# Sixty-four column products of a conditioning matrix shared out over three engines, in the filter stage of a gMLP/Hyena block

## The chip, the cores and the metric

One core of a Trainium2 chip. The metric is the device time in microseconds (us) of one execution; the runs before the change have a median of 2732.48 us (three runs, 2732.22 to 2733.73).

## The reference, cut to what matters

The block computes, for 512 tokens of width 2048 in float32:

```python
mod = silu(c) @ w_ada + b_ada                    # 6 vectors of 2048: sh1, sc1, g1, sh2, sc2, g2
h   = x * (1 + sc1) + sh1
z   = h @ w_in + b_in                            # 2048 -> 9216, then split
# Hyena branch: filters of length 512, made from positions alone
f   = sin(fr * (feats @ w1 + b1)); f = sin(fr * (f @ w2 + b2)); f = f @ w3
filt = f.reshape(L, 2, 2, 1024) * window         # direction, order, channel
y = x2 * conv(x1 * conv(v, filt0) + skip0, filt1) + skip1     # by a transform of length 1024
# then the gating branch, w_o, LayerNorm, a 2048 -> 8192 -> 2048 MLP, LayerNorm
```

All that the change touches lies before the first product with `w_in`: the vectors sh1 and sc1, the filters, and h.

## The kernel before, in words

**Number format.** A float32 product is made of float32r parts: a value is split into a high part (a cast on ScalarE, ACT) and a low part (value minus high, on VectorE, DVE), and three matmuls of high and low parts are added up. A block of weights (128x1024) so costs a cast (`whi`, L164) and a subtraction (`wlo`, L169), and the matmuls that take its low part wait for the subtraction.

**The modulation.** sh1 and sc1 aren't made on TensorE (PE). Each chunk of 128 columns, in two halves, is a tile `araw` of 128x1024; `Modulation.step` multiplies it with the broadcast silu(c) (`cond`) and adds up along the row, in one DVE instruction (L289, "a step" below). There are 64 steps for sh1 and sc1: 2 vectors, 16 chunks, 2 halves. After each fourth step one chunk of h can be made by `first_input`: two small POOL additions (`mod`, L295 and L296), two ACT instructions (the high part `act`, L476, and the full value in place in `xT`, L477), and one POOL subtraction (the low part, L478). So sixteen such chunks, kc 0 to 15.

**The filters.** Two sines (`Sine`: a matmul, an ACT scaling, `reduce` with six DVE instructions, an ACT Sin) give `a2`. Then eight parts, n = 0 to 7, each with three stages: `taps(n)` on PE (12 matmuls, and in even parts one more, L437, that adds the skip weight to the first tap), `windowed(n)` on DVE (four products of a PSUM bank with the window, L445), and `transform(n)` on PE (6 float32 matmuls, in the profile 12 rows: f_ee, f_eo, and two f_o of two matmuls each). The sums of part n (six DVE instructions, L376, L354 or L356, L380) read the transform's banks. PSUM has eight banks, used in turn: `taps` and `transform` have four each, so `transform(n)` overwrites what sums(n-1) read, and `taps(n+1)` what `windowed(n-1)` read. The loop over n issues taps(n+1), transform(n), two steps, windowed(n+1), the stores of the part before, the split of the next filter weights (`w3h`, `w3l`, each second part), sums(n).

**The first product.** Then two column groups of `w_in` are computed together, in sixteen blocks b0 to b15 of 24 matmuls; block b(2k) and b(2k+1) use the chunks kc 2k and 2k+1 of h. The loop over u = 0 to 15 issues on DVE: some of the remaining steps, all done by u = 12, then the `wlo` of block u+1; on PE: block u. In-order queues set all of this: every engine runs its instructions in the written order, and a waiting instruction holds up what stands behind it.

`busy(n)` issues n transposes of an identity whose result nobody reads. After u = 15 the program goes on with short convolutions, the other column groups and all the rest, which the change leaves as it is.

Of the kernel before, what the change touches and what calls it, by code (L numbers as in the profile page):

```python
# [11 lines left out]
F32 = mybir.dt.float32  # L12
F32R = mybir.dt.float32r
AF = mybir.ActivationFunctionType
OP = mybir.AluOpType
# [3 lines left out]
P = 128  # L19
# [21 lines left out]
def block_kernel(ctx: ExitStack, tc: tile.TileContext, t):  # L41
    nc = tc.nc
    const = ctx.enter_context(tc.tile_pool(name="const", bufs=1))
# [3 lines left out]
    small = ctx.enter_context(tc.tile_pool(name="small", bufs=2))  # L47
# [18 lines left out]

    def f32(ap):
        return ap.bitcast(F32)

    def load(dst, src, queue=nc.sync):  # L70
        queue.dma_start(dst, src)
        return dst

    def split(src, hi, lo):

        nc.scalar.copy(hi, src)
        nc.vector.tensor_tensor(lo, src, f32(hi), op=OP.subtract)
# [165 lines left out]
    cond = const.tile([P, D], F32, name="cond")  # L243
# [7 lines left out]
    sign = const.tile([P, 1], F32, name="sign")  # L251
    nc.gpsimd.memset(sign[:HID], 1.0)
    nc.gpsimd.memset(sign[HID:], -1.0)
    first_tap = const.tile([1, P], F32, name="first_tap")
    nc.gpsimd.memset(first_tap, 0.0)
    nc.gpsimd.memset(first_tap[:, 0:1], 1.0)
    ident = const.tile([P, P], F32, name="ident")
    make_identity(nc, ident)

    def busy(n):  # L260

        ps = bank("busy")
        for _ in range(n):
            nc.tensor.transpose(ps[:, :P], ident, ident)


    dots = const.tile([P, 6, KC, 2], F32, name="dots")
    mod = const.tile([P, 6, KC], F32, name="mod")

    class Modulation:  # L270
        def __init__(self, order, room=lambda: 0):

            self.order, self.raw, self.room = [(m, kc, h) for m, kc in order for h in range(2)], [], room

        def load(self):
            early = sum(r[0] for r in self.raw)
            more = early < min(self.room(), 8)
            if self.order and (more or len(self.raw) - early < 3):
                m, kc, h = self.order.pop(0)
                if more:  # L280
                    raw = actp.tile([P, 1024], F32, name="araw", tag="act")
                else:
                    raw = wts.tile([P, 1024], F32, name="araw", tag="araw")
                load(raw, t["ada"][m, kc, h])
                self.raw.append((more, raw, m, kc, h))

        def step(self):
            _, raw, m, kc, h = self.raw.pop(0)
            nc.vector.scalar_tensor_tensor(raw, raw, 1.0, cond[:, 1024 * h:1024 * (h + 1)], op0=OP.mult,  # L289
                                           op1=OP.mult, accum_out=dots[:, m, kc, h:h + 1])  # L290
            if len(self.raw) < 11:
                self.load()

    def mod_sum(m, kc, eng=nc.vector):
        eng.tensor_tensor(mod[:, m, kc], dots[:, m, kc, 0], dots[:, m, kc, 1], op=OP.add)  # L295
        eng.tensor_tensor(mod[:, m, kc], mod[:, m, kc], bada[:, m, kc], op=OP.add)  # L296
# [87 lines left out]
    PARTS = [(o, hf, cs) for o, hf in ((1, 1), (1, 0), (0, 0), (0, 1)) for cs in range(2)]  # L384

    class Filters:
# [6 lines left out]
        def middle(self):  # L393
            x = self.one.reduce()
            nc.scalar.activation(x, x, AF.Sin)
            self.two = Sine(hw2, x, 1, P)

        def ready(self):

            x = self.two.reduce()  # L400
            nc.scalar.activation(x, x, AF.Sin)
            even, odd = slot_pair("a2e"), slot_pair("a2o")
            split(x, *even)
            for a, b in zip(even, odd):
                nc.scalar.activation(b, f32(a), AF.Identity, scale=sign)
            self.a2 = [[a.rearrange("h (p k) -> h k p", k=4) for a in pair] for pair in (even, odd)]

        def fetch(self, n):

            o, hf, cs = PARTS[n]  # L410
            if cs == 0:
                w = load(slot("w3"), t["w3"][o, hf].rearrange("d h c -> (d h) c"))
                skip = load(slot("skip")[:1], t["skip"][o, hf:hf + 1])
                self.raw.append((w, skip))
            if n in (0, 2):
                for i in (2, 3) if hf else (0, 1):
                    self.win.append(load(actp.tile([P, 1024], F32, name="win", tag="act"), t["win"][i]))

        def parts(self, n):
            if PARTS[n][2] == 0:  # L420
                w, skip = self.raw.pop(0)
                both = slot_pair("w3")
                split(w, *both)
                self.w.append((*both, skip))

        def taps(self, n):

            cs = PARTS[n][2]
            wh, wl, skip = self.w[0] if cs == 0 else self.w.pop(0)
            ah, al = self.a2[cs]  # L430
            for cl in range(4):
                ps = bank("flt")
                extra = cs == 0 and cl == 0
                for m, (a, w) in enumerate(((ah, wh), (ah, wl), (al, wh))):
                    nc.tensor.matmul(ps, a[:, cl, :], w, start=m == 0, stop=m == 2 and not extra)  # L435
                if extra:
                    nc.tensor.matmul(ps, first_tap, skip, start=False, stop=True)  # L437
                self.ps.append(ps)

        def windowed(self, n):  # L440
# [27 lines left out]

    h1 = []

    def first_input(kc, xt):

        mod_sum(slice(0, 2), kc, nc.gpsimd)
        hi, lo = act_pair(kc)
        sc, sh = mod[:, 1, kc:kc + 1], mod[:, 0, kc:kc + 1]
        nc.scalar.activation(hi, xt, AF.Identity, bias=sh, scale=sc)  # L476
        nc.scalar.activation(xt, xt, AF.Identity, bias=sh, scale=sc)  # L477
        nc.gpsimd.tensor_tensor(lo, xt, f32(hi), op=OP.subtract)  # L478
        h1.append((hi, lo))

    def short_conv(ps, which, hf):
# [16 lines left out]
    ada = Modulation(((m, kc) for kc in range(KC) for m in range(2)), lambda: KC - 2 - len(h1) - 4 * bool(windows))  # L498
# [2 lines left out]
    bada = cload("bada", (P, 6, KC))  # L501
    flt = Filters()
    flt.fetch(0)
    silu = [slot("silu") for _ in range(4)]
    quarters = [cond[:, 512 * h:512 * (h + 1)] for h in range(4)]
    for s_, c_ in zip(silu, quarters):
# [6 lines left out]
    xt = []  # L513

    def x_load():
        if len(xt) < KC:
            xt.append(load(slot("xT"), t["xT"][len(xt)]))

    done = []

    def ada_steps(n):

        for _ in range(n):
            ada.step()
            done.append(None)
            if len(done) % 4 == 0:
                first_input(len(h1), xt[len(h1)])
                x_load()

    x_load()  # L530
    ada.load()
# [1 line left out]
    for m in (1, 4):  # L533
        nc.vector.tensor_scalar(bada[:, m], bada[:, m], 1.0, None, op0=OP.add)
    busy(14)
    ada_steps(2)
    flt.parts(0)
    flt.ready()
    busy(14)
    x_load()  # L540
    for _ in range(5):
        ada.load()
    flt.taps(0)
    ada_steps(2)
    flt.windowed(0)
    weights.later, weights.queue = [], nc.scalar
    for n in range(8):
        if n < 6 and n % 2 == 0:
            flt.fetch(n + 2)
        if n < 7:  # L550
            flt.taps(n + 1)
        sums = flt.transform(n)
        ada_steps(2)
        if n < 7:
            flt.windowed(n + 1)
        flt.store()
        if n < 6:
            flt.parts(n + 2)
        sums()
        if 2 <= n < 5:  # L560
            weights.load()
        if n == 5:
            weights.cast()
        if n == 6:
            weights.finish()
            weights.cast()
# [31 lines left out]
    for x in fc.tiles:  # L598
        both = slot_pair("fc")
# [111 lines left out]
    def do(f, *args):  # L711
        return lambda: f(*args)
# [52 lines left out]
    ada = Modulation((m, kc) for m in (2, 4, 3, 5) for kc in range(KC))  # L765
# [16 lines left out]
    for cg in range(4):  # L782
# [3 lines left out]
        ps = dense(t["w_b"], cg, 4, Bp)  # L786
# [56 lines left out]
    for hf in range(2):  # L843
# [77 lines left out]
    r = [[None] * 4 for _ in TILES]  # L921
# [100 lines left out]
    skips = []  # L1022

    w_o = t["w_o"]
    early, late = (0, 1), (2, 3)
# [213 lines left out]
```

## Time and profile before

| what | us |
|---|---|
| median of three runs | 2732.48 |
| the profiled execution | 2733.2 |
| its span, first to last instruction | 2731.4 |
| PE busy | 2688.6 (98%) |
| DVE busy | 1539.5 (56%) |
| ACT busy | 777.8 (28%) |
| POOL busy | 118.8 (4%) |
| mean granted TensorE clock | 0.996 |

The profiled execution lies 0.7 us above the median, and its span leaves 1.8 us around it. Rows of the timeline give the start of an instruction, its duration, engine, line, operation, output and inputs, how many follow each other, and in brackets how long the engine was idle before it and what ended that. Durations overlap a little at their ends (a step lasts 1.22 us and the next starts 1.15 us after it). PE rows with a wait on the memory of operands are modelled, so their starts are read, not their ends. All rows are the profile's, with the line numbers of the kernel before.

### The profile page before, as it was taken

The numbers are of one execution on the slowest core, as the hardware profiler recorded it, in microseconds if no ns is written. First come the engines' busy times: TensorE is split into PE (matmuls) and PEld (weight loads), VectorE is DVE, ScalarE is ACT, GpSimd is POOL, SyncE is SP. The second block draws the span as 40 slices with busy tenths as digits, with TensorE's granted clock in tenths as the row PEclk, the third lists the DMA queues.
The fourth block names the chain that finished last, engine by engine and source line by source line (L and its number), as shares of the span: only waits on it lengthen the run. The fifth ranks groups of instructions, "written<-read, shape, count | busy, mean of one in ns | idle before, by whom it ended". The sixth has DMA issues, their size and how long they took to land.

```text
span 2731.4 us, 30019 instructions
## 1 busy us (share of the span) xinstructions
PE 2688.6 (98%) x12019; PEld 2210.1 (81%) x12019; DVE 1539.5 (56%) x2052; ACT 777.8 (28%) x949; POOL 118.8 (4%) x102
## 2 busy tenths in 40 slices
PE   8999999999999999999999999999999999999996
PEld 5678778888888888878988888888888888888885
DVE  8987989544575566456774343443433434334348
ACT  2343332222232222324621222312223222131232
POOL 0330000000000000140010000000000000000001
PEclk9999999999999999999999999999999999999998
DMA  9762333555665567445543222322223222223342
GB/s 346 300 242 84 118 113 135 196 190 196 200 209 186 198 220 258 156 152 177 183 134 100 94 100 93 101 93 100 94 99 97 96 100 93 101 92 101 95 140 82
DMA packets 120189, 400.49 MB, mean 147 GB/s; under 512 B 14187, under 2 KB 14283, under 8 KB 119920
## 3 DMA queue, kind: packets, MB, share of 16 engines
q1 hardware_dynamic: 116656, 387.26, 41.9%
q10 hardware_dynamic: 3392, 11.31, 1.1%
q8 instruction: 94, 1.54, 0.2%
q14 instruction: 47, 0.39, 0.0%
HBM read 388.01 MB, written 10.50 MB: 146 GB/s over the span
## 4 chain that ended last, share of the span: by engine, by line
PE 91%; DVE 5%; DMA 3%; issue 1%; ACT 1%; SPq 0%; DVEq 0%; ACTq 0%
PE d L207 57%; PE t L952 29%; DMA araw<-in_ada 2%; PE flt L435 1%; PE f_o L338 1%; DVE wlo L169 1%; DMA spec<-spec 1%; PE inv L703 1%; PE inv L690 1%; DMA wraw<-in_w_m 0%; PE f L342 0%; DVE araw L289 0%; DVE r L1104 0%; DVE r L968 0%; PE tr L609 0%
## 5 line engine op out<-in xcount | busy, mean ns | idle before, releaser
L207 PE MATMUL d<-act,whi 128*128 128x512 f32 (+1 forms) x4224 | 1273.1, 384 | 0.0
L169 DVE TENSOR_TENSOR wlo<-wraw,whi 128x1024 fp32r<-128x1024 f32 x480 | 589.0, 1229 | 993.2 <-ACT whi L164 989.9
L164 ACT CAST whi<-wraw 128x1024 fp32r<-128x1024 f32 x480 | 504.9, 1053 | 1488.2 <-PE d L207 873.2
L207 PEld LDWEIGHTS d<-act,whi 128*128 128x128 f32 x4224 | 783.1, 188 | 155.6 <-issue 2.4
L207 PE MATMUL d<-act,wlo 128*128 128x512 f32 (+1 forms) x2112 | 810.2, 384 | 10.2 <-DVE wlo L169 10.2
L207 PEld LDWEIGHTS d<-act,wlo 128*128 128x128 f32 x2112 | 396.7, 188 | 93.3 <-DVE wlo L169 15.9
L952 PE MATMUL t<-whi,fh 128*128 128x512 f32 x960 | 373.5, 389 | 0.0
L952 PE MATMUL t<-wlo,fh 128*128 128x512 f32 x960 | 373.5, 389 | 0.0
L952 PE MATMUL t<-whi,fl 128*128 128x512 f32 x960 | 373.5, 389 | 0.0
L289 DVE SCALAR_TENSOR_TENSOR araw<-araw,cond 128x1024 f32<-128x1024 f32 x192 | 238.6, 1259 | 7.8 <-DMA araw<-in_ada 7.6
L952 PEld LDWEIGHTS t<-whi,fl 128*128 128x128 f32 x960 | 180.2, 188 | 37.4
L952 PEld LDWEIGHTS t<-whi,fh 128*128 128x128 f32 x960 | 180.2, 188 | 37.4
L952 PEld LDWEIGHTS t<-wlo,fh 128*128 128x128 f32 x960 | 180.2, 188 | 37.4
L952 PE MATMUL t<-whi,act 128*128 128x512 f32 x512 | 159.7, 391 | 0.0
L952 PEld LDWEIGHTS t<-whi,act 128*128 128x128 f32 x512 | 96.1, 188 | 19.9
L967 DVE TENSOR_TENSOR gated<-t,cond 128x512 f32<-128x512 f32 x126 | 86.2, 684 | 31.6 <-PE t L952 31.6
L952 PE MATMUL t<-wlo,act 128*128 128x512 f32 x256 | 99.8, 390 | 2.1 <-DVE wlo L169 2.1
L968 DVE TENSOR_TENSOR r<-r,gated 128x512 f32<-128x512 f32 x126 | 87.2, 692 | 4.3
L207 PE MATMUL d<-whi,act 128*128 128x512 f32 x256 | 79.0, 389 | 0.0
L1062 DVE TENSOR_TENSOR relu<-relu 128x512 f32<-128x512 f32 (+1 forms) x68 | 45.6, 671 | 38.2 <-ACT fh L1061 38.2
L1106 POOL TENSOR_TENSOR r<-r,ln2b 128x512 f32<-128x512 f32 x6 | 10.0, 1665 | 1305.1 <-DVE r L1104 1303.8
L952 PEld LDWEIGHTS t<-wlo,act 128*128 128x128 f32 x256 | 48.1, 188 | 12.3 <-DVE wlo L169 2.5
(253 smaller groups left out, 1966.9 us busy)
## 6 DMA issues: line engine op xcount, KB each, us to landing
wraw<-in_w_m SPq DMA_DIRECT2D x264, 512.0 KB, 3.5
araw<-in_ada SPq DMA_DIRECT2D x192, 512.0 KB, 5.7
wraw<-in_w_in SPq DMA_DIRECT2D x123, 512.0 KB, 3.6
wraw<-in_w_o SPq DMA_DIRECT2D x48, 512.0 KB, 3.4
spec<-spec SPq DMA_DIRECT2D x48, 256.0 KB, 4.0
wraw<-in_w_in ACTq DMA_DIRECT2D x21, 512.0 KB, 6.7
wraw<-in_w_b SPq DMA_DIRECT2D x16, 512.0 KB, 3.6
wraw<-in_w_a SPq DMA_DIRECT2D x16, 512.0 KB, 3.4
```

Of the source, the lines that this page charges most:

```text
L164: nc.scalar.copy(hi, raw)
L169: nc.vector.tensor_tensor(lo, raw, f32(hi), op=OP.subtract)
L207: nc.tensor.matmul(out[i], a, b, start=first and m == 0, stop=last and m == 2)
L289: nc.vector.scalar_tensor_tensor(raw, raw, 1.0, cond[:, 1024 * h:1024 * (h + 1)], op0=OP.mult, op1=OP.mult, accum_out=dots[:, m, kc, h:h + 1])
L338: nc.tensor.matmul(ps, fc(k), x, start=first, stop=last)
L435: nc.tensor.matmul(ps, a[:, cl, :], w, start=m == 0, stop=m == 2 and not extra)
L690: nc.tensor.matmul(ps, ic(4 * cs + COLUMN[cl]), y[cl][cs], start=(cs == 0), stop=(cs == 1))
L703: nc.tensor.matmul(ps[:, cl * P:(cl + 1) * P], conv.y[cl][cs][:, s], ic(4 * cs + COLUMN[cl]), start=(cs == 0), stop=(cs == 1))
L952: nc.tensor.matmul(out[i], a, b, start=kc == 0 and m == 0, stop=kc == 2 * pairs - 1 and m == 2)
L967: nc.vector.tensor_tensor(x, ps[i], g2_row[c], op=OP.mult)
L968: nc.vector.tensor_tensor(r[i][c], r[i][c], x, op=OP.add)
L1062: nc.vector.tensor_tensor(x, x, x, op=OP.mult)
```

## The change

1. Of the 64 steps, 19 become two instructions: `products` multiplies on POOL (L302 of the new kernel), `add_up` copies the product in place on ACT and adds up along the row (L309). Two products are issued before the loop, then two or three in each part up to n = 6; the sums on ACT stand at the head of the next part. Six more stay DVE steps before the loop, none inside it. When the loop ends 25 steps are done (before: 20), and 39 remain for the first product (before: 44): three per u instead of three or four.
2. The small additions of `first_input` run on DVE where `add_up` triggers them, on POOL otherwise; the low part of h moves from POOL to DVE (L510). It is put in a list (`lows`) and issued by `low()`: after the next step, in the filter loop behind `windowed`.
3. The second sine's `reduce` is issued before the split of the filter weights and after one step, not after two; its Sin is computed twice on ACT, once straight into the high part.
4. `busy(14)` before the first taps becomes `busy(36)`.
5. The four skip rows are loaded once, into partitions 0, 32, 64 and 96 of one tile, split once on ACT and DVE, and added by two float32r matmuls in place of one float32 matmul.

The DVE queue around the first taps and windows, before. Names: `araw` a step, `w3l` the low part of filter weights, `a2el` that of the sines, `flt` the windowed taps:

```order
L289 SCALAR_TENSOR_TENSOR araw,dots<-araw,cond 128x1024 x2
L77 TENSOR_TENSOR w3l<-w_122,w3h 128x512
L316 TENSOR_SCALAR sine_k<-sine 128x512
L317 TENSOR_SCALAR sine_k<-sine_k 128x512
L319 SCALAR_TENSOR_TENSOR sine<-sine_k,sine 128x512 x3
L320 TENSOR_SCALAR sine<-sine 128x512
L77 TENSOR_TENSOR a2el<-sine,a2eh 128x512
L289 SCALAR_TENSOR_TENSOR araw,dots<-araw,cond 128x1024 x2
L445 TENSOR_TENSOR flt<-flt,win 128x512 x4
```

The same stretch now, from the same place of the program (`skipl` is the low part of the skips, `act_303` the low part of chunk 0 of h):

```order
L293 SCALAR_TENSOR_TENSOR araw,dots<-araw,cond 128x1024
L336 TENSOR_SCALAR sine_k<-sine 128x512
L337 TENSOR_SCALAR sine_k<-sine_k 128x512
L339 SCALAR_TENSOR_TENSOR sine<-sine_k,sine 128x512 x3
L340 TENSOR_SCALAR sine<-sine 128x512
L77 TENSOR_TENSOR w3l<-w_126,w3h 128x512
L293 SCALAR_TENSOR_TENSOR araw,dots<-araw,cond 128x1024
L426 TENSOR_TENSOR a2el<-sine,a2eh 128x512
L77 TENSOR_TENSOR skipl<-skip,skiph 97x512
L293 SCALAR_TENSOR_TENSOR araw,dots<-araw,cond 128x1024 x3
L510 TENSOR_TENSOR act_303<-xT,act_303 128x512
L293 SCALAR_TENSOR_TENSOR araw,dots<-araw,cond 128x1024
```

Behind it stand the four windowed products. Between `a2el` and these there were two steps; now there are the skips' split, three steps, the low part of chunk 0 and a fourth step.

The DVE queue in the first product, u = 1 to 3, before:

```order
L289 SCALAR_TENSOR_TENSOR araw,dots<-araw,cond 128x1024 x3
L169 TENSOR_TENSOR wlo<-wraw,whi 128x1024
L289 SCALAR_TENSOR_TENSOR araw,dots<-araw,cond 128x1024 x4
L169 TENSOR_TENSOR wlo<-wraw,whi 128x1024
L289 SCALAR_TENSOR_TENSOR araw,dots<-araw,cond 128x1024 x3
L169 TENSOR_TENSOR wlo<-wraw,whi 128x1024
```

And now, u = 1 to 3:

```order
L293 SCALAR_TENSOR_TENSOR araw,dots<-araw,cond 128x1024
L510 TENSOR_TENSOR act_863<-xT,act_863 128x512
L293 SCALAR_TENSOR_TENSOR araw,dots<-araw,cond 128x1024 x2
L169 TENSOR_TENSOR wlo<-wraw,whi 128x1024
L293 SCALAR_TENSOR_TENSOR araw,dots<-araw,cond 128x1024 x2
L510 TENSOR_TENSOR act_951<-xT,act_951 128x512
L293 SCALAR_TENSOR_TENSOR araw,dots<-araw,cond 128x1024
L169 TENSOR_TENSOR wlo<-wraw,whi 128x1024
L293 SCALAR_TENSOR_TENSOR araw,dots<-araw,cond 128x1024 x3
L510 TENSOR_TENSOR act_1010<-xT,act_1010 128x512
L169 TENSOR_TENSOR wlo<-wraw,whi 128x1024
```

The low part of a chunk of h stands between the steps, one step behind the step that completes the chunk.

```diff
     class Modulation:
...
+        def products(self, n):
+            for _ in range(n):
+                _, raw, m, kc, h = item = self.raw.pop(0)
+                nc.gpsimd.tensor_tensor(raw, raw, cond[:, 1024 * h:1024 * (h + 1)], op=OP.mult)
+                self.half.append(item)
+
+        def add_up(self):
+            n = len(self.half)
+            while self.half:
+                _, raw, m, kc, h = self.half.pop(0)
+                nc.scalar.activation(raw, raw, AF.Copy, accum_out=dots[:, m, kc, h:h + 1])
+                if len(self.raw) < 11:
+                    self.load()
+            return n
...
         def ready(self):
-            x = self.two.reduce()
+            x, even, odd = self.x, slot_pair("a2e"), slot_pair("a2o")
+            nc.scalar.activation(even[0], x, AF.Sin)
             nc.scalar.activation(x, x, AF.Sin)
-            even, odd = slot_pair("a2e"), slot_pair("a2o")
-            split(x, *even)
+            nc.vector.tensor_tensor(even[1], x, f32(even[0]), op=OP.subtract)
...
+        def skips(self):
+            self.skip = [x[:97] for x in slot_pair("skip")]
+            split(skip_raw, *self.skip)
...
                 if extra:
-                    nc.tensor.matmul(ps, first_tap, skip, start=False, stop=True)
+                    for m, x in enumerate(self.skip):
+                        nc.tensor.matmul(ps, first_tap[row:row + 1], x[row:row + 1], start=False, stop=m == 1)
...
-    def first_input(kc, xt):
+    def first_input(kc, xt, eng):
-        mod_sum(slice(0, 2), kc, nc.gpsimd)
+        mod_sum(slice(0, 2), kc, eng)
...
-        nc.gpsimd.tensor_tensor(lo, xt, f32(hi), op=OP.subtract)
+        lows.append(lambda: nc.vector.tensor_tensor(lo, xt, f32(hi), op=OP.subtract))
...
+    def counted(n, eng):
+        for _ in range(n):
+            done.append(None)
+            if len(done) % 4 == 0:
+                first_input(len(h1), xt[len(h1)], eng)
+                x_load()
+
     def ada_steps(n):
+        if not n:
+            low()
         for _ in range(n):
             ada.step()
-            done.append(None)
-            if len(done) % 4 == 0:
-                first_input(len(h1), xt[len(h1)])
-                x_load()
+            low()
+            counted(1, nc.gpsimd)
...
-    ada_steps(2)
+    ada_steps(1)
+    flt.reduced()
     flt.parts(0)
+    ada_steps(1)
     flt.ready()
-    busy(14)
+    flt.skips()
+    busy(36)
...
     flt.taps(0)
     ada_steps(2)
+    ada.products(2)
+    ada_steps(2)
+    low()
     flt.windowed(0)
...
     for n in range(8):
...
+        counted(ada.add_up(), nc.vector)
         if n < 7:
             flt.taps(n + 1)
         sums = flt.transform(n)
-        ada_steps(2)
         if n < 7:
+            ada.products(2 + n % 2)
             flt.windowed(n + 1)
+        low()
         flt.store()
```

More of the change, by code (lines that the diff above doesn't have):

```diff
@@ L253, in block_kernel @@
     nc.gpsimd.memset(sign[HID:], -1.0)
-    first_tap = const.tile([1, P], F32, name="first_tap")
-    nc.gpsimd.memset(first_tap, 0.0)
-    nc.gpsimd.memset(first_tap[:, 0:1], 1.0)
+    first_tap = const.tile([97, P], F32R, name="first_tap")
+    one_hot = small.tile([97, P], F32, name="one_hot", tag="one_hot")
+    nc.gpsimd.memset(one_hot, 0.0)
+    nc.gpsimd.memset(one_hot[:, 0:1], 1.0)
+    nc.vector.tensor_copy(first_tap, one_hot)
+    skip_raw = slot("skip")[:97]
+    nc.gpsimd.memset(skip_raw, 0.0)
     ident = const.tile([P, P], F32, name="ident")
@@ L271, in __init__ @@
         def __init__(self, order, room=lambda: 0):
-            self.order, self.raw, self.room = [(m, kc, h) for m, kc in order for h in range(2)], [], room
+            self.order, self.raw, self.half, self.room = [(m, kc, h) for m, kc in order for h in range(2)], [], [], room
         def load(self):
-            early = sum(r[0] for r in self.raw)
+            early = sum(r[0] for r in self.raw + self.half)
             more = early < min(self.room(), 8)
-            if self.order and (more or len(self.raw) - early < 3):
+            if self.order and (more or len(self.raw + self.half) - early < 3):
                 m, kc, h = self.order.pop(0)
@@ L396, in middle, with reduced @@
             self.two = Sine(hw2, x, 1, P)
+        def reduced(self):
+            self.x = self.two.reduce()
         def ready(self):
-            x = self.two.reduce()
+            x, even, odd = self.x, slot_pair("a2e"), slot_pair("a2o")
+            nc.scalar.activation(even[0], x, AF.Sin)
             nc.scalar.activation(x, x, AF.Sin)
-            even, odd = slot_pair("a2e"), slot_pair("a2o")
-            split(x, *even)
+            nc.vector.tensor_tensor(even[1], x, f32(even[0]), op=OP.subtract)
             for a, b in zip(even, odd):
@@ L411, in fetch @@
             if cs == 0:
-                w = load(slot("w3"), t["w3"][o, hf].rearrange("d h c -> (d h) c"))
-                skip = load(slot("skip")[:1], t["skip"][o, hf:hf + 1])
-                self.raw.append((w, skip))
+                self.raw.append(load(slot("w3"), t["w3"][o, hf].rearrange("d h c -> (d h) c")))
             if n in (0, 2):
@@ L420, in parts @@
             if PARTS[n][2] == 0:
-                w, skip = self.raw.pop(0)
                 both = slot_pair("w3")
-                split(w, *both)
-                self.w.append((*both, skip))
+                split(self.raw.pop(0), *both)
+                self.w.append(both)
+        def skips(self):
+            self.skip = [x[:97] for x in slot_pair("skip")]
+            split(skip_raw, *self.skip)
         def taps(self, n):
-            cs = PARTS[n][2]
-            wh, wl, skip = self.w[0] if cs == 0 else self.w.pop(0)
+            o, hf, cs = PARTS[n]
+            wh, wl = self.w[0] if cs == 0 else self.w.pop(0)
+            row = 32 * (2 * o + hf)
             ah, al = self.a2[cs]
@@ L469, in block_kernel, with low @@
     h1 = []
-    def first_input(kc, xt):
-        mod_sum(slice(0, 2), kc, nc.gpsimd)
+    lows = []
+    def low():
+        while lows:
+            lows.pop(0)()
+    def first_input(kc, xt, eng):
+        mod_sum(slice(0, 2), kc, eng)
         hi, lo = act_pair(kc)
@@ L503, in block_kernel @@
     flt.fetch(0)
+    for k in range(4):
+        load(skip_raw[32 * k:32 * k + 1], t["skip"][k // 2, k % 2:k % 2 + 1])
     silu = [slot("silu") for _ in range(4)]
```

## The prediction

> **What bounds the kernel now.** I read the waits of PE over the whole run first, to see which stretch can give or lose time at all.
>
> ```profile
> PE d L207 <- DVE wlo L169: 10.2, 10, 2.6
> ```
>
> (us in total, times, longest.) 10.2 us, nearly all PE ever waits for another engine once the filters run, is for the low part of a weight block in the first product. Behind it PE is fed, so the change moves the end by what it moves the last of these waits. PE's timeline gives the marks:
>
> ```profile
> 19.60 0.62 PE L435 MATMUL flt<-w3h,a2eh 128*128 128x512 f32 x1 [3.03 <-ACT a2eh L76]
> ...
> 34.83 0.80 PE L435 MATMUL flt<-w3h,a2eh 128*128 128x512 f32 x1
> ...
> 91.91 1.02 PE L207 MATMUL d<-act,whi 128*128 128x512 f32 x2
> ...
> 101.05 0.50 PE L207 MATMUL d<-act,wlo 128*128 128x512 f32 x1 [2.64 <-DVE wlo L169]
> ...
> 174.36 0.50 PE L207 MATMUL d<-act,wlo 128*128 128x512 f32 x1 [1.39 <-DVE wlo L169]
> ```
>
> The first taps start at 19.60; transform(0) ends at 34.83, where the next taps begin; transform(7) at 91.91, where block b0 begins; b13 gets its low part at 174.36. From 34.83 to 91.91 PE has no gap; from 101 to 174 DVE paces it: twelve blocks in 73.3 us, 6.1 each, where PE needs 5.5 (24 matmuls in the chain of waits):
>
> ```profile
> 204.71 5.47 PE d L207 x24
> ```
>
> The window view of 100 to 110 (PE, PEld, DVE, ACT, POOL busy, clock, DMA share) shows DVE full, and the transfers full too:
>
> ```profile
> 100.00:110.00 10.00, 8.95 (x39) 7.43 (x40) 10.00 (x13) 2.57 (x3) 4.75 (x4) 1.00 1.03 414
> DVE araw L289 <- DMA araw<-in_ada: 2.4, 4, 1.1
> ```
>
> DVE waited only 2.4 us for transfers; three steps per block instead of 3.4 ask for less. Transfers stay off the sum.
>
> **The change, part by part.** Prices on DVE:
>
> ```profile
> 22.69 0.69 DVE L445 TENSOR_TENSOR flt<-flt,win 128x512 f32<-128x512 f32 x1
> ...
> 29.75 2.48 DVE L445 TENSOR_TENSOR flt<-flt,win 128x512 f32<-128x512 f32 x4
> 32.89 0.69 DVE L77 TENSOR_TENSOR w3l<-w,w3h 128x512 fp32r<-128x512 f32 x1 [0.66 <-ACT w3h L76]
> ...
> 96.35 1.22 DVE L289 SCALAR_TENSOR_TENSOR araw<-araw,cond 128x1024 f32<-128x1024 f32 x1
> ```
>
> Durations overlap by their tails: four windowed products take 2.4, so one DVE instruction of 128x512 0.6, and the six sums of a part 3.6; a step 1.15 and a `wlo`, as wide, 1.14.
>
> *POOL beside DVE.* This decides most of it:
>
> ```profile
> 22.92 0.20 POOL L296 TENSOR_TENSOR mod<-mod,c_bada 128x2 f32<-128x2 f32 x1
> 24.89 1.28 POOL L478 TENSOR_TENSOR act<-xT,act 128x512 fp32r<-128x512 f32 x1 [1.77 <-ACT xT L477]
> ...
> 102.22 1.11 POOL L295 TENSOR_TENSOR mod<-dots 128x2 f32<-128x2 f32 x1 [5.87 <-DVE araw L289]
> 103.42 1.07 POOL L296 TENSOR_TENSOR mod<-mod,c_bada 128x2 f32<-128x2 f32 x1
> 106.26 1.60 POOL L478 TENSOR_TENSOR act<-xT,act 128x512 fp32r<-128x512 f32 x1 [1.78 <-ACT xT L477]
> ```
>
> ```profile
> 106.64 2.31 DVE L289 SCALAR_TENSOR_TENSOR araw<-araw,cond 128x1024 f32<-128x1024 f32 x1
> ```
>
> An addition of two columns takes 0.20 alone, but 1.11 beside a step: it waits for that step's end. At 106.26 POOL waits for the step that ends at 106.64, runs its 1.2 us, and the next step, there since 106.64, takes 2.31 instead of 1.22. They exclude each other, and the one that waits goes next. At 24.89 DVE worked on windowed taps, one input in PSUM, and nothing stretched. So only DVE work with both inputs in SBUF (steps, `w3l`, `wlo`, low parts) meets a product. A product of 1024 columns: from 0.20 for two and 1.28 for 512, about 2.4 us; above, twice 1.28, 2.56. The Trainium skill (SBUF — State Buffer, section "SBUF: two separate sides") says that the pair of ports is an exclusive lock held for the whole instruction; no run here shows that for 2.4 us yet, and the sum below takes it from the rows.
>
> *The start.* ACT and PE:
>
> ```profile
> 12.42 0.78 ACT L312 ACTIVATE sine<-flt,hfb,c_hcol 128x512 f32<-128x512 f32 x1 [2.16 <-PE flt L311]
> ...
> 18.27 0.63 ACT L401 ACTIVATE sine<-sine 128x512 f32<-128x512 f32 x1 [4.57 <-DVE sine L320]
> 18.93 0.62 ACT L76 CAST a2eh<-sine 128x512 fp32r<-128x512 f32 x1
> ```
>
> ```profile
> 12.31 4.27 PE L264 MATMUL busy<-ident 128*128 128x128 f32 x28
> ```
>
> A step and `w3l`, 1.75, no longer stand ahead of the reduction; since the scaling is there only at 13.2, 1.5 of that is won: the Sin at 16.8, and with no cast behind it the high part at 17.4, 2.15 earlier. The 22 more transposes, at the mean of the 28 (0.15), last to 19.9 at most, so the taps start 17.4 to 19.9; nothing hangs on it, because windowed(0) comes later than both. DVE's queue from 16.75: `w3l` to 17.35, a step to 18.5, `a2el` to 19.1; ACT then scales (0.7) and casts the skips (0.6), 20.5; their low part 21.1; three steps, 24.55, of which the second (23.4) completes chunk 0. Its low part now waits on DVE: POOL's first addition waits for the third step (23.4 + 1.27), the second ends at +1.56, ACT's two take 1.7 (the 1.78 that POOL waits for them ahead of 106.26), so the low part can start at +3.3, 26.7. By then POOL, done with its additions at 24.95, is in the first product, until 27.4: low part 27.5 to 28.1. The second product has been waiting and goes next, to 30.5; the fourth step behind it ends at 31.65, and there windowed(0) begins. Before, it began at 22.69, as soon as there were taps. Now PE has the skips at 21.1 and the 21 matmuls left of both taps at 0.234 (2.81 for 12, below) done by 26.4, and waits to about 32.3, when the first window is through: 5.9 us.
>
> PE's prices, in the chain of waits:
>
> ```profile
> 36.09 1.05 PE flt L437 x2
> ...
> 39.59 0.86 PE f_ee L338 x2
> 40.45 0.86 PE f_eo L338 x2
> 41.31 3.43 PE f_o L338 x8
> 44.74 2.81 PE flt L435 x12
> ```
>
> *The clock.* Windows of PE alone (busy, clock, DMA share):
>
> ```profile
> 21.00:22.00 1.00, 1.00 (x2) 0.60 1.02 401
> ...
> 28.00:29.00 1.00, 1.00 (x6) 0.98 1.03 410
> ```
>
> After the 3.03 us gap ahead of 19.60 the clock was near half for 7 us; after the 2.64 us at 101 it stayed at 1.00. So 5.9 us costs the clock, and what the added transposes keep warm goes cold again on transform(0), which is on the path. Its work is 0.86 + 0.86 + 3.43 = 5.15 us. Started at 32.3 and paced by the windows it ends at 37.8 with a warm clock, at 40.9 after 7 us at half; I take 39.5, since the restart may have begun a slow period late, as at 19.60. By the Trainium skill (TensorE: Matmul & The Clock Gate, Part 1), one busy window of about 3.4 us brings the clock back: an end at 39.1 by that rule. So transform(0) ends 4.7 later. Below: if the second product doesn't come between and the gap stays short, windowed(0) is at 28.5 and transform(0) ends at 34.3, 0.5 earlier.
>
> *The loop.* The skip's two matmuls at 0.234 each replace 1.05 (L437), three times behind part 0: −1.7 us. DVE's load falls to 6.0 per part plus 0.6 to 1.4 for low parts and additions, under PE's 5.15 + 2.81 = 8.0, so PE paces. Against that, POOL has no pacing of its own: 17 products in a row, 2.4 each, from 31.7 to past 72. In each part where DVE has a low part and a `w3l`, each can wait up to 2.4. Walking parts 2 and 4 so, PE loses 0 (none met) to 2.8 us (all met): 0.8. ACT's sums (nearest row: a 128x1024 cast, 1.05, plus reading the sum) fill 3 of 8 us and hide. transform(7): 91.91 + 4.7 − 1.7 + 0.8 = 95.7. DVE ends the sums of part 7 two subtractions behind it, 97.0 (before 96.35; two steps stood ahead of them).
>
> *The first product.* Now 13 times three steps, a `wlo`, and in nine of them a low part of h, up to the `wlo` of b13. Steps 39 × 1.147 = 44.7; `wlo` 13 × 1.14 = 14.8; low parts 9 × 0.6 = 5.4. And the waits: where one step stands between, the low part can start at +3.3 and DVE arrives at +1.15: 2.15. Where a `wlo` and a step stand between (each fourth block), both additions wait for DVE (1.11 and 1.07, the rows above), +4.15 against +2.29: 1.86. Behind the waiting low part stand the steps and the `wlo` that PE waits for. Six times 2.15 and three times 1.86: 18.5. Together 83.4; before, 174.30 − 96.35 = 77.95, with 44 steps, and POOL's subtraction costing DVE about 1.1 a chunk. The five steps saved and the lock removed are smaller than the new waits. `wlo` of b13: 97.0 + 83.4 = 180.4, PE 180.5, against 174.36: **+6.1 us**. The last chunk's low part falls behind that, under b13's 5.5 us.
>
> Sum: the profiled 2733.2 + 6.1 = 2739.3; the median lies 0.7 below the profiled, so 2738.5.
>
> **The rivals.** (a) *The waits hide*: the low parts find `xT` ready. Then DVE needs 64.9 for 13 blocks, PE 71.5, and PE paces: 95.7 + 71.6 = 167.3, −7: 2725.5. For it: DVE loses 14 of 20 steps from the filters, as intended. Against: the queue has one step between, and the rows give +3.3.
> (b) *The start isn't hurt*: transform(0) at 34.3, no met products: transform(7) at 89.7, `wlo` of b13 at 91.0 + 83.4, PE at 174.5: no change, 2732.6. It needs the fourth step to slip ahead of the second product; the rows at 106 say the waiting one goes next.
> (c) *POOL becomes the bound of the filters*: from 3.5 us per product, 19 take until 91.5, and DVE's additions in the last part wait for ACT's sums: first product at 99.5, +8.6, 2741. The locks it gives way to count too. Against: 2.56 at most by the rows. It is the case of my own sign.
>
> **How the numbers follow.** Forecast 45%, (a) 15%, (b) 23%, (c) 17%. 0.2% is 5.5 us, so slower begins at 2738.0. The forecast's own range, from its waits ± 0.3 each (2.7) and the clock (−1.7 to +1.4), straddles this: 25 points slower, 20 same. (a): 13 faster, 2 same. (b): 3 faster, 18 same, 2 slower. (c): slower. Faster 0.16, same 0.40, slower 0.44. Range: below, (b) less 2.7, 2729; above, 40.9 and all products met with 2.7 more, +12: 2744.
>
> **What would show it.** windowed(0) starting near 31 to 32, a second product ahead of it; PE idle 5 to 6 us before the first f_ee, and the granted clock near half behind it; low parts of h in the first product with 1.8 to 2.2 us idle ahead, put down to ACT `xT`; b13's low part near 180. If b13 stands before 172, (a) is right and the walk of DVE's queue wrong. If the clock stays 1.00 from 30 to 40, the start's term is too large by 1.7. If products last beyond 3.5 us with no DVE work beside them, (c).

## The result, and the profile after

The changed kernel takes 2759.36 us (median of four runs, 2756.30 to 2761.64); the kernel before, run beside it, 2733.11. The ratio is 1.0093, with a 95% interval of 1.0075 to 1.0110: **slower by about 26 us**, where the prediction said 6. The profiled execution takes 2761.0 us, its span is 2759.2.

The waits of PE over the whole run of the changed kernel (us in total, times, longest):

```profile
PE d L207 <- DVE wlo L169: 14.7, 11, 2.5
PE flt L460 <- DVE w3l L77: 8.3, 2, 4.6
PE f_ee L358 <- DVE flt L471: 7.2, 1, 7.2
```

Only the first line has a counterpart before (10.2). The two others are new, and both lie in the filters. PE's timeline after, and the last row that has the same place in every version, PE's last wait for a `wlo` in this product, of the kernel before and after:

```profile
34.09 2.08 PE L358 MATMUL f_ee<-flt,fwd 128*128 128x512 f32 x2 [7.18 <-DVE flt L471]
...
43.05 0.62 PE L460 MATMUL flt<-w3h,a2eh 128*128 128x512 f32 x1 [1.35 <-ACT w3h L76]
48.25 0.81 PE L460 MATMUL flt<-w3l,a2eh 128*128 128x512 f32 x1 [4.58 <-DVE w3l L77]
72.38 0.79 PE L460 MATMUL flt<-w3l,a2eh 128*128 128x512 f32 x1 [3.77 <-DVE w3l L77]
...
113.88 1.02 PE L207 MATMUL d<-act,whi 128*128 128x512 f32 x2
```

```profile
198.47 0.50 PE L207 MATMUL d<-act,wlo 128*128 128x512 f32 x1 [1.19 <-DVE wlo L169]
```

```profile
225.78 0.50 PE L207 MATMUL d<-act,wlo 128*128 128x512 f32 x1 [1.19 <-DVE wlo L169]
```

Two marks carry the rest: **b0**, the first row of the first product (91.91 before, 113.88 after, +22.0), and the **last mark** (198.47, 225.78, +27.3). The filters lost 22 us, the first product 5.3, and behind that nothing: the span grew by 27.8.

What stretched DVE from 24 to 48 us, in order:

```profile
24.12 3.27 DVE L293 SCALAR_TENSOR_TENSOR araw<-araw,cond 128x1024 f32<-128x1024 f32 x1 [0.73 <-DMA araw<-in_ada]
27.33 2.82 DVE L510 TENSOR_TENSOR act<-xT,act 128x512 fp32r<-128x512 f32 x1
30.07 3.36 DVE L293 SCALAR_TENSOR_TENSOR araw<-araw,cond 128x1024 f32<-128x1024 f32 x1
33.36 2.47 DVE L471 TENSOR_TENSOR flt<-flt,win 128x512 f32<-128x512 f32 x4
35.76 2.21 DVE L315 TENSOR_TENSOR mod<-dots 128x2 f32<-128x2 f32 x1
38.00 2.27 DVE L316 TENSOR_TENSOR mod<-mod,c_bada 128x2 f32<-128x2 f32 x1
40.19 2.47 DVE L471 TENSOR_TENSOR flt<-flt,win 128x512 f32<-128x512 f32 x4
42.58 2.87 DVE L510 TENSOR_TENSOR act<-xT,act 128x512 fp32r<-128x512 f32 x1
45.37 2.82 DVE L77 TENSOR_TENSOR w3l<-w,w3h 128x512 fp32r<-128x512 f32 x1
```

POOL meanwhile runs one product behind the other:

```profile
23.91 33.50 POOL L302 TENSOR_TENSOR araw<-araw,cond 128x1024 f32<-128x1024 f32 x13
```

Everything here with both inputs in SBUF takes nearly a product longer than its own time (2.1 to 2.2 us): a subtraction of 128x512 2.8 in place of 0.69, even an addition of two columns 2.2. The windowed products, one input in PSUM, keep their 2.47 for four. PE stands at the end of this queue: the taps of part 2 need `w3l`, behind a step, two additions and two low parts.

### The profile page after: what moved, and what is told of

It reads as the page before. It is cut to its first block, busy times and chain, and to the rows that moved or that the text cites. A ratio compares the mean times of both kernels' runs of the same rounds, so it can differ in the third digit from the quotient of the medians.

```text
span 2759.2 us, 30066 instructions
## 1 busy us (share of the span) xinstructions
PE 2696.9 (98%) x12041; PEld 2216.0 (80%) x12041; DVE 1545.1 (56%) x2042; ACT 798.4 (29%) x988; POOL 132.5 (5%) x96
## 4 chain that ended last, share of the span: by engine, by line
PE 89%; DVE 6%; DMA 2%; issue 1%; ACT 1%; POOL 0%; SPq 0%; DVEq 0%; ACTq 0%; POOLq 0%
PE d L207 57%; PE t L1001 28%; DVE araw L293 1%; DVE wlo L169 1%; PE flt L460 1%; DMA araw<-in_ada 1%; PE f_o L358 1%; PE inv L752 1%; PE inv L739 0%; DMA wraw<-in_w_m 0%; PE f L362 0%; DVE r L1017 0%; DVE gated L1016 0%; DVE act L510 0%; DVE st L1019 0%
## 5 line engine op out<-in xcount | busy, mean ns | idle before, releaser
L293 DVE SCALAR_TENSOR_TENSOR araw<-araw,cond 128x1024 f32<-128x1024 f32 x173 | 212.8, 1243 | 5.3 <-DMA araw<-in_ada 5.3
```

## The experiments

Each kernel ran with the kernel before beside it (medians of 2733.9 to 2735.0). Times are medians; the two marks come from the one profiled execution of each kernel, which took up to 5.2 us more than the median (e2). Edits are to the changed kernel unless it is said otherwise.

| run | time | ratio to before | b0 | last mark |
|---|---|---|---|---|
| before | 2733.11 | 1 | 91.91 | 198.47 |
| the change | 2759.36 | 1.0093 (1.0075–1.0110) | 113.88 | 225.78 |
| e1 products on DVE | 2751.36 | 1.0059 (1.0044–1.0074) | 99.46 | 214.99 |
| e2 halved products | 2747.48 | 1.0049 (1.0034–1.0064) | 103.61 | 215.59 |
| e3 additions on POOL | 2746.02 | 1.0040 (1.0025–1.0055) | 98.41 | 208.23 |
| e4 late low parts | 2747.11 | 1.0048 (1.0031–1.0064) | 109.68 | 209.64 |
| e5 steps, late low parts | 2740.45 | 1.0019 (1.0009–1.0028) | 93.24 | 203.04 |
| e6 before, late low parts | 2736.93 | 1.0007 (0.9998–1.0017) | 91.72 | 200.67 |
| e7 PE kept warm | 2758.30 | 1.0084 (1.0069–1.0099) | 110.06 | 222.05 |
| e8 = e3 + e4 | 2731.30 | 0.9986 (0.9977–0.9996) | 98.83 | 195.05 |
| e9 = e8, window first | 2734.26 | 0.9997 (0.9988–1.0006) | 101.64 | 197.84 |
| e10 = e9, halved products | 2730.19 | 0.9984 (0.9975–0.9994) | 96.37 | 192.62 |
| e11 = e6, five loads less | 2735.72 | 1.0002 (0.9993–1.0012) | 91.89 | 198.02 |
| e12 = e10, w3 earlier | 2727.29 | 0.9976 (0.9966–0.9985) | 95.20 | 191.41 |
| e13 before, late low in product | 2735.53 | 1.0004 (0.9995–1.0013) | 91.81 | 198.23 |

### e1: products on DVE

```
-                nc.gpsimd.tensor_tensor(raw, raw, cond[:, 1024 * h:1024 * (h + 1)], op=OP.mult)
+                nc.vector.tensor_tensor(raw, raw, cond[:, 1024 * h:1024 * (h + 1)], op=OP.mult)
```

> The change with its products on VectorE in place of POOL; ScalarE's sums, the additions of two columns on VectorE, the low parts and the start stay. Theory (a product on POOL holds up every VectorE instruction with both inputs in SBUF for its full 2.4 us, and PE then waits for the low part w3l and goes cold): the additions L315/L316 and w3l lose their waits, at 0.1 to 0.7 us each; VectorE has some 9.5 us of work per part against 8 of PE, so it paces instead, transform(7) ends near 101 to 103 in place of 113.9, and the time is about 2748 (2744 to 2752). Rival (ScalarE's sums come late and with them the loads that they trigger, whoever multiplies): PE's idle time before the even taps stays, 2757 or more.

b0 came 14.4 us earlier, though DVE now has 19 products more; the last mark 10.8, since b1's `wlo` then stands behind a full DVE and PE waits 5.3 us for it. Groups on DVE from 19 to 98 us (busy, mean ns), of the change and then of e1:

```profile
L510 DVE TENSOR_TENSOR act<-xT,act 128x512 fp32r<-128x512 f32 x5 | 9.7, 1930 | 0.0
L293 DVE SCALAR_TENSOR_TENSOR araw<-araw,cond 128x1024 f32<-128x1024 f32 x4 | 9.0, 2268 | 0.7 <-DMA araw<-in_ada 0.7
L77 DVE TENSOR_TENSOR w3l<-w,w3h 128x512 fp32r<-128x512 f32 x3 | 6.3, 2112 | 0.2 <-ACT w3h L76 0.2
L316 DVE TENSOR_TENSOR mod<-mod,c_bada 128x2 f32<-128x2 f32 x4 | 4.9, 1222 | 0.1
L315 DVE TENSOR_TENSOR mod<-dots 128x2 f32<-128x2 f32 x4 | 3.2, 800 | 0.0
```

```profile
L293 DVE SCALAR_TENSOR_TENSOR araw<-araw,cond 128x1024 f32<-128x1024 f32 x4 | 4.8, 1220 | 0.0
L510 DVE TENSOR_TENSOR act<-xT,act 128x512 fp32r<-128x512 f32 x5 | 3.4, 684 | 0.7 <-ACT xT L509 0.7
L77 DVE TENSOR_TENSOR w3l<-w,w3h 128x512 fp32r<-128x512 f32 x3 | 2.1, 686 | 0.0
L316 DVE TENSOR_TENSOR mod<-mod,c_bada 128x2 f32<-128x2 f32 x4 | 0.7, 163 | 0.1
L315 DVE TENSOR_TENSOR mod<-dots 128x2 f32<-128x2 f32 x4 | 0.6, 157 | 0.0
```

The differences, at the counts shown: low parts 6.3, steps 4.2, `w3l` 4.2, additions 4.2 and 2.6, together **21.5 us of waiting in DVE**. This is nearly the 22.0 lost at b0, but a wait of DVE costs only where PE stands behind it; what the run shows is that 14.4 of the 22.0 hang on where the products run. ScalarE's sums and the loads behind them are the same in both, so the rival falls. What e1 still lacks at b0 (7.6) goes with DVE's own work: DVE is busy for 59.5 of the 60 us from 38 to 98. The Trainium skill (SBUF — State Buffer, section "SBUF: two separate sides") calls the shared ports an exclusive lock for the whole instruction, against DVE work with two SBUF inputs; these rows agree, for instructions of 2.4 us.

### e2: halved products

```
-                nc.gpsimd.tensor_tensor(raw, raw, cond[:, 1024 * h:1024 * (h + 1)], op=OP.mult)
+                for q in range(2):
+                    r, c = raw[:, 512 * q:512 * (q + 1)], cond[:, 1024 * h + 512 * q:1024 * h + 512 * (q + 1)]
+                    nc.gpsimd.tensor_tensor(r, r, c, op=OP.mult)
```

> The change with every product on POOL cut in two of 512 columns: the same elements, twice the instructions. Theory (a VectorE instruction with both inputs in SBUF waits for the product that runs, to its end): each such wait falls from some 2.2 us to some 1.2; transform(7) ends near 106 (103 to 109), the time is about 2751. Rival (what costs is POOL's work beside VectorE as such, or ScalarE's sums and the transfers, not the length of one instruction): unchanged or a little longer than the change, 2759 to 2763.

The last mark came 10.2 us earlier, b0 10.3: it is the length of one instruction that counts, not the work on POOL. b0 lies in the expected range, and the time 3.5 below the expected 2751, although in the profiled execution one addition broke the rule. DVE and POOL of e2:

```profile
68.78 6.82 DVE L317 TENSOR_TENSOR mod<-dots 128x2 f32<-128x2 f32 x1
```

```profile
61.94 13.64 POOL L304 TENSOR_TENSOR araw<-araw,cond 128x512 f32<-128x512 f32 x11
```

It waited for the half that ran and five more, to the end of POOL's run at 75.58. That a waiting instruction always goes next, as the prediction read from two rows, is wrong; it did so elsewhere, and when it does not stays open.

### e3: additions on POOL

```
-        counted(ada.add_up(), nc.vector)
+        counted(ada.add_up(), nc.gpsimd)
```

> The change with the additions of two columns that follow ScalarE's sums moved from VectorE to POOL, as they are in the first product. Theory (each of the two additions of a chunk waits for one product on VectorE, 2.2 us): both waits are gone from VectorE, and POOL, which has them ahead of its next products and must wait for ScalarE's sums first, pauses and lets w3l and the low part pass; transform(7) near 106, the time near 2751. Rival (the additions only wait where VectorE would have waited for POOL anyway, at w3l or the low part behind them): 2757 to 2760.

Better than expected: b0 earlier by 15.5. The additions are gone from DVE (8.1 us), and PE's two waits for `w3l` shrank from 8.3 to 1.1 us, so the clock stayed up behind them. Low parts (1.80 on the mean) and `w3l` (1.56) still wait: POOL runs five products in a row, then waits for ScalarE's sums, in which time DVE passes. The additions' 8.1 us are about half of the 15.5; the pauses that a queued addition gives POOL and the clock may make up the rest, but this run doesn't separate them.

### e4: late low parts

```
             ada.step()
-            low()
+            if windows or len(done) % 4 == 2:
+                low()
```

`windows` is empty in the first product only, so the filters stay as they are.

> The change with the low part of each chunk of h recorded two steps later in the first product, the filters untouched. Theory (the low part waits 1.8 to 2.1 us for ScalarE's xT, nine times, with VectorE idle and the steps and wlo that PE waits for behind it): no such wait, VectorE needs some 65 us for thirteen blocks and PE paces with its 71.5; b13's low part near 190 to 191 in place of 200.7, the time about 2749.5. Rival (the transfers, whose share is 1.03 there, pace as soon as VectorE does not): waits of araw or wraw for DMA take the place, 2754 to 2758.

As expected, and 2.4 us better: of the 16.1 us at the mark, 4.2 came ahead of b0, which this edit doesn't touch (2.0 of it stands already at the first f_ee, 32.05 against 34.09; e3 and e8, which are alike up to there, differ by 1.1), and 11.9 behind it. In the change, and in e4, a low part and what follows:

```profile
134.16 0.69 DVE L510 TENSOR_TENSOR act<-xT,act 128x512 fp32r<-128x512 f32 x1 [2.06 <-ACT xT L509]
```

```profile
121.94 0.69 DVE L510 TENSOR_TENSOR act<-xT,act 128x512 fp32r<-128x512 f32 x1
122.54 1.22 DVE L169 TENSOR_TENSOR wlo<-wraw,whi 128x1024 fp32r<-128x1024 f32 x1
```

PE has no wait at all from 118.64 to 202.71 in e4. The nine waits decided the first product, not the transfers.

### e7: is it the clock?

```
                 extra = cs == 0 and cl == 0
+                if (n, cl) in ((1, 3), (2, 0), (4, 0)):
+                    for _ in range(44):
+                        nc.tensor.transpose(ps[:, :P], ident, ident)
```

> The change with 44 more identity transposes on PE in each of three places where it waits and then runs at half clock: ahead of the last bank of taps(1), of taps(2) and of taps(4), into the bank that those taps write next. Theory (a third of the filters' loss is the clock: three stretches of some 7 us at half behind the waits of 7.2, 4.6 and 3.8 us): clock near 1.00 in them, transform(7) some 8 us earlier, 2751 (2748 to 2754). Rival (VectorE behind POOL's products paces the parts, and PE's slow stretches hide behind it): 2758 to 2760.

PE's windows behind the second wait (PE, PEld, DVE, ACT, POOL busy, clock, DMA share), of the change and of e7:

```profile
46.00:50.00 4.00, 1.75 (x3) 1.04 (x4) 3.97 (x4) 0.00 (x0) 4.00 (x2) 0.50 0.00 0
50.00:54.00 4.00, 4.00 (x10) 2.80 (x9) 3.55 (x7) 0.00 (x0) 4.00 (x3) 0.50 0.65 238
```

```profile
46.00:50.00 4.00, 4.00 (x32) 4.00 (x31) 3.96 (x4) 0.00 (x0) 4.00 (x2) 0.88 0.00 0
50.00:54.00 4.00, 4.00 (x16) 3.10 (x15) 4.00 (x7) 0.00 (x0) 4.00 (x3) 1.00 0.52 192
```

The clock was kept up, and 3.7 us came of it at the mark, half of what the theory asked for. The time, 2758.30, lies where the rival has it, and its interval overlaps that of the change. So the rival holds in the main: DVE, full in the same rows, paces, and half or more of PE's slow stretches hides behind it. By the mark the clock is a seventh of the loss, by the time less.

### e8, e9, e10, e12: towards a better version

e8 is e3 and e4 together.

> The change with the additions of two columns back on POOL and the low parts of the first product two steps later, both single edits together. Theory (the two losses stand one behind the other, b0 at 98.4 and PE paced behind it): the gains of 13.3 and 12.3 us add up to the point where VectorE paces again: b13 near 170, 2736 (2733 to 2739). Rival (one hides the other): no better than 2744.

Better than expected, and faster than the kernel before: from 105.65 to 188.12 PE waits for nothing, and from b0 to the last mark it takes 96.2 us, against 106.6 before and 111.9 in the change. That more than pays for the 6.9 still lost at b0.

e9 records windowed(0) ahead of products and steps:

```
     ada_steps(2)
+    flt.windowed(0)
     ada.products(2)
     ada_steps(2)
     low()
-    flt.windowed(0)
```

> The kernel with both edits (additions on POOL, late low parts) and one more: windowed(0) is recorded ahead of the first two products and of the third and fourth step, so it stands in VectorE's queue behind the second step as in the kernel before plus one. Theory (what is left of the loss stands at the start: PE's 5 us idle ahead of the first f_ee and the half clock behind it): no such wait, b0 near 93 in place of 98.8, PE fed behind it, the time about 2725.5 (2722 to 2728). Rival (the two steps and the products then stand ahead of windowed(1), and PE waits there instead): 2730 or more.

The theory fell, and e9 is slower than e8. PE's wait ahead of f_ee is gone, but the next one came, and not where the rival had it; the clock then stood at 0.50 from 38 to 46:

```profile
37.47 0.82 PE L460 MATMUL flt<-w3h,a2eh 128*128 128x512 f32 x1 [5.08 <-ACT w3h L76]
40.23 0.82 PE L460 MATMUL flt<-w3l,a2eh 128*128 128x512 f32 x1 [1.94 <-DVE w3l L77]
```

e10 is e9 with the products halved as in e2.

> The same with every product cut in two of 512 columns. Theory (w3l, the low parts and the steps of the start still wait for a whole product each, 1.1 us of PE's idle time before taps(4) among it): another 1 to 3 us less, about 2723.5. Rival (behind the additions on POOL there are no waits left that PE sees, and 19 more instructions make POOL longer): the same as the run beside it, or up to 2 more.

b0 came 5.3 us earlier and the time is 4.1 less, more than the expected 1 to 3, with no wait for `w3l` left and the wait for `w3h` unchanged (5.27). The 2723.5 that the expectation counted from e9's forecast was not reached. ACT's row of e10 names the cause of the wait:

```profile
37.13 0.62 ACT L76 CAST w3h<-w 128x512 fp32r<-128x512 f32 x1 [2.41 <-DMA w<-in_w]
```

e12 issues this load ahead of the five `araw` blocks:

```
-            if cs == 0:
+            if cs == 0 and n != 2:
...
+    flt.raw.append(load(slot("w3"), t["w3"][1, 0].rearrange("d h c -> (d h) c")))
     for _ in range(5):
         ada.load()
```

> The last version (additions on POOL, late low parts, windowed(0) first, halved products) with the load of part 2's w3 issued ahead of the five araw blocks of the start instead of behind eight of them. Theory (PE's 5.3 us ahead of taps(2) are a transfer, w from in_w, that stands in the queue behind araw blocks while the transfers are full): the wait goes, b0 near 91.5 in place of 96.4, PE fed from there, about 2726 (2723 to 2728). Rival (the araw blocks, then later, delay the steps and with them windowed(1), which takes the wait over): 2729.5 to 2731.

The wait fell to 2.8, and 1.4 for `w3l` took part of its place; the time is 2727.29, ratio 0.9976 (0.9966 to 0.9985), within the expected range, though b0 (95.20) is not near 91.5. It is the fastest version here: PE is fed through the first product, and its b0 is 3.3 behind the kernel before.

### e5, e6, e11, e13: the kernel before and its first product

e5 takes products and sums out altogether (two steps a part, low parts two steps late everywhere); e6 and e13 edit the kernel before alone.

> The change without any product on POOL or sum on ScalarE: two steps a part on VectorE as before, the low parts of h on VectorE but two steps later throughout; sine chain, more transposes and the split skips stay. Theory (products beside VectorE and the waits for xT are the whole loss; the rest of the change gains a little): b0 near 90, VectorE with the subtractions at 0.6 in place of POOL's lock of 1.1 needs some 6 us less up to b13, the time is about 2726 (2723 to 2729). Rival (the later windowed(0), with the skips' low part and a step ahead of it, or the low parts between the windows, take it back): 2731 or more.

> The kernel before with one edit: the low part of each chunk of h on VectorE, two steps later, in place of POOL. Theory (POOL's subtraction of 128x512 costs VectorE about 1.1 by the lock, VectorE itself needs 0.6, and 14 of them stand ahead of b13): 5 to 7 us less, 2728 (2726 to 2730). Rival (transfers are full in the first product, share 1.03, and pace as soon as VectorE is faster): 2731 to 2733.

Both theories missed: e6 gained nothing and e5 is 5.4 us slower than the kernel before. In e5 the later windowed(0) is not the cause. transform(0) ends at 32.57, 2.3 ahead of the kernel before; PE then waits 2.32 for `w3h`, whose load comes late as in e9 (ACT is idle 5.32 for it), and the clock is 0.59 from 38 to 42. In the first product e5 loses what e6 loses: PE waits 5.90 for b1's `wlo`. In e6, b1's `wlo`, behind low parts that DVE now does in the filters, comes 2.7 us later than before (102.44 against 99.78), and PE waits 5.5 us for it and runs at 0.71 of its clock behind it. PE's row and the window of e6:

```profile
103.72 0.79 PE L207 MATMUL d<-act,wlo 128*128 128x512 f32 x1 [5.52 <-DVE wlo L169]
```

```profile
102.00:112.00 10.00, 8.29 (x28) 6.67 (x29) 10.00 (x15) 2.58 (x3) 2.98 (x3) 0.71 1.03 414
```

Either that took the gain, or the transfers did (share 1.03). e11 takes five loads out of e6, e13 leaves the filters as before:

> The kernel before with late low parts on VectorE, and with five of its araw blocks not loaded: the step multiplies the block before once more (so five of the products are of the wrong rows; VectorE has as many instructions as without that edit). Theory (transfers, not VectorE, pace the first product once POOL's subtractions are gone; the five blocks of 0.5 MB that the change takes out of it ahead of time are worth 1.3 us each at 405 GB/s): PE's waits behind 150 us go, 2731.5 (2729.5 to 2733.5) against 2737. Rival (VectorE's number of steps paces): unchanged, 2736 to 2738.

> The kernel before with the low parts of h on VectorE, two steps later, in the first product only; in the filters they stay on POOL. Theory (POOL's subtraction does cost VectorE 1.1 a chunk in the first product, but with the edit throughout the filters' low parts made VectorE late for b1, whose wait grew from 2.64 to 5.5 and took the clock to half behind it, some 5.8 together): b1's wait back near 2.6 with the clock at 1.00, the time 2731.5 (2729 to 2733). Rival (transfers, full there, take what VectorE wins, as its 10.1 us of waits for araw in place of 2.4 suggest): 2734.5 to 2737.

The 10.1 us in the last expectation is a total over the whole run, where the kernel before has 7.6; from 96 to 178 it is 4.3 in e6 and 2.4 before. e11 gave 2.7 us at the mark, but 1.2 in time, which the intervals don't tell from nothing; it lies between its two expectations. e13 meets its rival: b1's wait is back to 2.67, and nothing is gained. The clock didn't stay at 1.00 behind that wait (0.83 on the mean of 102 to 112), but PE has no further wait up to 147.47, so this doesn't set b13. PE's rows at b1 and b13 in e13, and the window of 142 to 152 of the kernel before and then of e13:

```profile
100.95 0.50 PE L207 MATMUL d<-act,wlo 128*128 128x512 f32 x1 [2.67 <-DVE wlo L169]
...
174.10 0.50 PE L207 MATMUL d<-act,wlo 128*128 128x512 f32 x1 [1.60 <-DVE wlo L169]
```

```profile
142.00:152.00 10.00, 10.00 (x43) 8.02 (x44) 9.52 (x14) 3.13 (x4) 5.80 (x5) 1.00 1.03 406
```

```profile
142.00:152.00 10.00, 9.30 (x42) 7.36 (x41) 8.08 (x17) 3.09 (x4) 1.59 (x4) 1.00 1.03 407
```

From b1 to b13 it takes 73.2 us, as before (73.3), though DVE now has 1.9 us to spare in these 10; the transfers have none. DVE's rows up to b13 say why. POOL's subtractions had lengthened eight steps of the kernel before by 7.8 us in all; e13's ten low parts cost DVE 6.0 in their place. Of the 1.8 won, the waits for `araw` took 2.0 (4.4 in place of 2.4). So the relief was small, and with 44 steps to go, each with a block of 0.5 MB, what there was went into loads; e11's 2.7 at the mark, without five of the loads, points the same way. With 39 steps (e4, e8) neither DVE nor the transfers hold PE up: from b0 to the last mark e8 takes 96.2 us, e13 with the same late low parts 106.4. So taking five steps out of the first product was worth its aim, and moving the low parts alone was not.

## Why the prediction was wrong

The direction was the likeliest case's, the size was a quarter of the result, and the range (2729 to 2744) missed it by 15 us. At the `wlo` of b13 (180.4 forecast, 200.67 measured) the 20.3 us divide into 2.2 in the start, 16.0 in the loop, 2.9 in the sums of part 7, and -0.8 in the first product.

- **The start: mechanism right, 2 us short.** windowed(0) began at 33.36 (31.65 forecast), PE waited 7.2 us (5.9), the clock was 0.50 from 34 to 38, transform(0) ended at 41.7 (39.5). The order was not the walk's: the third step waited 0.73 for its block, so POOL's additions and its first product went ahead (23.91), and that step met the product, where the walk had left it free. The low part then met the second product, and the fourth step a third one, which the walk had behind windowed(0). So there were three meetings in place of two; that the products began 1 us early made up for a part. ACT's sums of the first two products show where these end:

```profile
26.35 1.06 ACT L309 ACTIVATE araw<-araw 128x1024 f32<-128x1024 f32 x1 [0.69 <-POOL araw L302]
...
29.63 1.06 ACT L309 ACTIVATE araw<-araw 128x1024 f32<-128x1024 f32 x1 [2.13 <-POOL araw L302]
```

- **The loop: the step that failed.** "Walking parts 2 and 4 so, PE loses 0 (none met) to 2.8 us (all met): 0.8." From transform(0) to b0 it took 72.2 us, where 56.2 were forecast: +16. PE waited 9.7 (1.35, 4.58 and 3.77) in place of 0.8, and behind the last two waits its clock was 0.50 from 48 to 55 and from 73 to 79, which by an estimate from these rows is some 7 us of work lost. Three things were left out. The additions of two columns, which the change moves onto DVE, were counted as work and not as instructions that can wait, though the prediction quoted one, then on POOL, at 1.11 beside a step; they waited 6.8 us in all. `w3l`, the low part and the additions stand in one queue ahead of the taps that need `w3l`, so their waits add up and are not set against PE's slack. And the clock behind PE's waits was priced in the start alone; e7, which kept it up in all three places, got only 3.7 back, since DVE paces behind it.
- **The sums of part 7: 2.9 us more.** The forecast has DVE done with them at 97.0, 1.3 behind transform(7); in the run it is 118.11, 4.2 behind it. A low part of h stands ahead of these sums, and it waited for `xT` there too:

```profile
113.80 0.69 DVE L510 TENSOR_TENSOR act<-xT,act 128x512 fp32r<-128x512 f32 x1 [1.78 <-ACT xT L509]
```

- **POOL's price: right.** 2.4 was taken, 2.58 is the mean spacing of the thirteen products, with the turns DVE takes among them. Rival (c), which asked for 3.5, is out; but POOL's unpaced row of products was the trouble, by what it locks and not by the time that it takes in all.
- **The first product: right.** From the step behind sums(7) to the end of b13's `wlo` 83.4 were forecast; 118.11 to 200.67 is 82.6, with low parts that wait 1.77 and 2.06 (1.86 and 2.15 forecast):

```profile
118.11 1.22 DVE L293 SCALAR_TENSOR_TENSOR araw<-araw,cond 128x1024 f32<-128x1024 f32 x1
...
199.53 1.22 DVE L169 TENSOR_TENSOR wlo<-wraw,whi 128x1024 fp32r<-128x1024 f32 x1
```

- **Transfers off the sum: right for the change, too easily argued.** In the changed kernel DVE's waits for `xT` came first (e4). The argument, that DVE waited only 2.4 us for loads, took a full DVE for the one bound where the share of 1.03 pointed to a second one close to it (e13).
- **The skips: right in kind, 0.5 us too large.** From the first matmul of taps(6) to f_ee, without a wait, it takes 4.20 in e8 (76.77 to 80.97) and 4.60 before (69.45 to 74.05): 0.4 a part and 1.2 for three, where 1.7 were forecast. In e5 the wait for `w3h` and the clock behind it hide this gain.
- **Rival (a), no waits, PE paces,** is what e4 made of the first product; rival (b) is what e9 made of the first f_ee, but its wait moved to the next load.

## What to carry to other kernels

Work given to POOL to relieve DVE is not free where DVE's instructions have both inputs in SBUF: count each such instruction, however small, as one that may wait for a whole POOL instruction, and add the waits up along the queue to the one that another engine needs. If the work must go there, cut it into short instructions, let something on POOL wait now and then, and keep small glue work in POOL's own queue. An engine at 100% beside transfers at a share of 1.03 can be two bounds that lie close together: what was taken off DVE alone went into waits for loads (e13), and what was taken off both came through (e8).

## What the runs showed of the hardware

- An addition of 128x2 took 0.16 us on DVE alone (e1) and 2.2 beside POOL products (the change), as long as a wide one waits.
- A waiting DVE instruction isn't always next: once five POOL instructions of 1.2 us in a row went ahead of it (6.82 us, e2).
- Identity transposes alone brought the granted clock from half to full: 0.69 on the mean of 42 to 46 us, 0.88 on that of 46 to 50, and 1.00 behind (e7; two of its windows are above, and its 44 transposes run from 43.00 to 49.69).
- The length of a wait doesn't settle by itself whether the clock falls: behind waits of 2.47 us (the change, b1) and 2.67 us (e13, b1, the row at 100.95) it fell, behind one of 2.64 us (before, b1, the row at 101.05) it did not. The Trainium skill (TensorE: Matmul & The Clock Gate, Part 1) says that the window in which the hardware watches PE's activity is free-running and doesn't reset when a kernel starts; these rows agree with that. PE's row of the change, its window behind it, the window of e13, and that of the kernel before:

```profile
122.83 0.50 PE L207 MATMUL d<-act,wlo 128*128 128x512 f32 x1 [2.47 <-DVE wlo L169]
```

```profile
124.00:126.00 2.00, 2.00 (x7) 1.52 (x6) 0.31 (x1) 1.97 (x3) 0.00 (x0) 0.50 0.98 389
```

```profile
102.00:112.00 10.00, 10.00 (x38) 8.08 (x37) 10.00 (x18) 3.80 (x5) 4.37 (x4) 0.83 1.03 412
```

```profile
103.00:105.00 2.00, 2.00 (x10) 1.69 (x9) 2.00 (x5) 0.48 (x1) 1.41 (x2) 1.00 1.04 424
```
